# One transformer layer on one core: the pairs of a seven-product scheme in four stages instead of three, each engine's order rewritten, a fourth raw buffer, the residual in DRAM during the MLP

## The chip, the cores and the metric

The kernel runs on one core of a Trainium2 chip. A core has several engines that run their own queues side by side: TensorE (PE, matrix products; PEld is its loading of the stationary operand), VectorE (DVE), ScalarE (ACT), GpSimd (POOL) and SyncE (SP, which here issues the loads), with 16 DMA engines behind the queues. The metric is the device time of one execution in microseconds, as the median of several runs. A further execution is taken by the hardware profiler; its page and its trace are what the profile means below.

## The reference

One layer of a decoder on a sequence of 256 tokens of width 2048, all in float32: a block-sparse attention and a short convolution, merged by gates, then a squared-ReLU MLP, then a gated input embedding.

```python
D_MODEL = 2048; SEQ = 256; D_FF = 4 * D_MODEL
...
        r = r + merged @ w_o[i]
        h = rms_norm(r, g_mlp[i])
        r = r + jnp.square(jax.nn.relu(h @ w_up[i])) @ w_down[i]
        h = rms_norm(r, g_ple[i])
        r = r + jax.nn.sigmoid(h @ w_ple_gate[i]) * (p[i] @ w_ple_proj[i])
```

The change concerns the third line and what stands directly before and behind it: `w_up` is 2048 x 8192 and `w_down` 8192 x 2048.

## The kernel before

**Products in parts.** A float32 operand is split into a high part, which ACT rounds to the matmul's format (`hi`, a Copy), and a low part, which DVE gets by subtraction (`lo`). A product is hi·hi + hi·lo + lo·hi. So every weight passes through ACT and DVE before PE can use it, and a `lo` waits for its `hi` (`split`, L115 to L122). All operations go through four helpers, whose lines the profile shows: `act` L77, `mm` L80, `load` L83, DVE L87.

**Units.** The MLP works in 96 units of 1 MB of weights (128 x 2048 elements, as two halves of 128 x 1024). 64 are `up` units, one for each 128 columns of `w_up`; 32 are `dn` units, for the upper half of `w_down`'s output columns (tiles 8 to 15), in four groups of eight, one group for each quarter of the hidden width. A unit takes 32 matmuls (`cols`, L202): 15 of 512 columns, 16 of 256, and one more of 512. The order is 17 up, 8 dn, 16 up, 8 dn, 16 up, 8 dn, 15 up, 8 dn (`units`, L464 to L467). Units are numbered 0 to 95; the loop body that issues unit g's matmuls is called body g here.

**Pairs.** The other half of `w_down`'s work (output tiles 0 to 7) is done by a scheme of seven products instead of eight on 2 x 2 blocks. A pair j takes two hidden tiles, 2j and 2j + 1, as the blocks A11 to A22, and a raw tile `raw_s` with four blocks of `w_down`, B. From the A blocks come four sums S1 to S4 (`sum_u`, L539: four DVE operations on a quarter tile, then a split). From the B blocks come T1 to T4: `t13` is one DVE subtraction on a whole half tile, `t24` an addition and a subtraction. What is split are B11 with B22 (`b`), B21, T1 with T3 (`t13`), T2 with T4 (`t24`) and S. Each of the seven products is three matmuls, and all 32 pairs add up in seven banks of PSUM, 0 to 6, from the first pair to the last. So from unit 3 on all units use the one bank left, 7: unit g + 1 can start on PE once ACT has copied unit g's sums out of it (`evacuated`, L570: the instructions `up<-ps_up` and `dn<-ps_dn`).

**The preparation of a pair** has three parts (`split_part`, L508): part 0 splits `b`, forms and splits the S, and subtracts for `t13`; part 1 splits `t13`, forms `t24` and splits B21; part 2 splits `t24`. A table made ahead, `after` (L471 to L477), deals out one part to a body, two from body 88 on, each three units after the later of its hidden tiles at the earliest; the products of a part (two, two, three; `pair_part`, L555) follow the unit of the body it is dealt to.

**What sets the order.** From body 2 on ACT, DVE, PE and SP run the program in the order it is written (`keep_in_program_order`); POOL does too. A body g (L624 to L661) issues, in this order: the load of unit g + 3; the load of a pair where one begins in body g + 3; the matmuls of unit g; the split of the first half of unit g + 2; the finishing of unit g - 1 (`up_done`, L575: two DVE operations form `a`, ACT squares it, ACT and DVE split it into `x`; or `dn_done`, L589); the parts dealt to body g + 1; the split of the second half of unit g + 2; the evacuation of unit g; and the products of the parts dealt to body g. A load waits until one of three `raw` buffers (1 MB each, shared by units and pairs) is free, and the loads behind it on SP wait with it.

**The residual r** is held in eight tiles. After w_o four of them, tiles 0 to 3, are stored to DRAM (`r_kept`, L448), to make room, and come back behind the last product (L660). Tiles 4 to 7 stay in SBUF: a dn unit of the first three groups adds its two halves to them by two DMAs of POOL that accumulate in flight (L592), the second of which waits for the first. The last group adds on DVE. The small tiles (x, sums, evacuated sums, r) share a pool of 50 slots, `N_SLOT`; a slot is given again when its last reader is done, so an evacuation can come to wait for such a DMA. The seven `hi` and seven `lo` buffers of half a unit are shared by units and pairs alike.

Of the kernel before, what the change touches and what calls it, by code (L numbers as in the profile page):

```python
# [15 lines left out]
N_SLOT = 50  # L16
P = 128
S = 256
# [18 lines left out]
def hybrid_block_kernel(ctx: ExitStack, tc: tile.TileContext, ins: dict, out: bass.AP):  # L37
# [76 lines left out]

    def split(hi, lo, src, gain=None):  # L115
# [8 lines left out]
    def xsplit(xs, k, src, gain=None):  # L124

        x = slot([P, 2, S], F32R, "x")
        split(x[:, 0, :], x[:, 1, :], src, gain)
        xs[k] = x
# [18 lines left out]
    def load_unit(w):  # L147

        raw = wp.tile([P, UNIT], F32, tag="raw", name="raw", bufs=3)
        load(raw, w)  # L150
        return [split_half(raw[:, h * HALF:(h + 1) * HALF]) for h in range(2)]

    def load_half(w):
        raw = wp.tile([P, HALF], F32, tag="raw", name="raw", bufs=3)
        load(raw, w)
        return split_half(raw)

    def load_rows(w):

        raw = wp.tile([P, UNIT], F32, tag="raw", name="raw", bufs=3)  # L160
# [62 lines left out]
    def temp(name):  # L223
        return sm.tile([P, S], F32, tag="temp", name=name, bufs=8)
# [33 lines left out]
    def load_first(w):  # L258

        raw = wp.tile([P, UNIT], F32, tag="raw", name="raw", bufs=3)  # L260
# [144 lines left out]
    def split_m(n, ps):  # L405
        for i in range(2):
            xsplit(mT, n + i, ps[:, i, :])
# [33 lines left out]
    r_kept = [dram.tile([P, 2, S], F32, tag=f"r{u}", name=f"r_kept_{u}") for u in range(4)]  # L441
# [36 lines left out]
    assert not todo  # L478

    def load_raw(g):  # L480
        if g < NU:
            kind, i = units[g]
            w = ins["w_up"][i] if kind == "up" else ins["w_down"][16 * i[0] + i[1]]
            wU[g] = [wp.tile([P, UNIT], F32, tag="raw", name="raw", bufs=3)]
            load(wU[g][0], w)

    def split_unit(g, h):
        if g < NU:
            raw = wU[g][0]
            wU[g].append(split_half(raw[:, h * HALF:(h + 1) * HALF]))  # L490
# [12 lines left out]

    def both(w, names, hi, lo):
        for i, name in enumerate(names):
            w[name] = hi[:, i * CW:(i + 1) * CW], lo[:, i * CW:(i + 1) * CW]

    def split_part(j, i):  # L508


        w = wS[j]
        if i == 0:
            raw = w["raw"]
            hi, lo = half_tiles("b")
            flat = raw[:, 0:2, :].rearrange("p a f -> p (a f)")
            split(hi, lo, flat)
            both(w, ("B11", "B22"), hi, lo)
            sum_u(j)
            t = wp.tile([P, 2, CW], F32, tag="t", name="t13", bufs=2)
            dve.tensor_sub(t, raw[:, 0:2, :], raw[:, 2:3, :].to_broadcast([P, 2, CW]))  # L520
            w["t13"] = t
        elif i == 1:
            raw, t = w["raw"], w["t13"]
            hi, lo = half_tiles("t13")
            split(hi, lo, t.rearrange("p a f -> p (a f)"))
            both(w, ("T1", "T3"), hi, lo)
            t2 = wp.tile([P, 2, CW], F32, tag="t", name="t24", bufs=2)
            dve.tensor_add(t2[:, 0, :], raw[:, 1, :], t[:, 0, :])
            dve.tensor_sub(t2[:, 1, :], t2[:, 0, :], raw[:, 3, :])
            hi, lo = (slot([P, CW], F32R, f"b21_{n}") for n in range(2))  # L530
            split(hi, lo, raw[:, 3, :])
            w["B21"] = hi, lo
            w["t24"] = t2
        else:
            hi, lo = half_tiles("t24")
            split(hi, lo, w["t24"].rearrange("p a f -> p (a f)"))
            both(w, ("T2", "T4"), hi, lo)

    def sum_u(j):  # L539
# [7 lines left out]
        hi, lo = (slot([P, 4, P], F32R, f"s_{i}") for i in range(2))  # L547
        split(hi, lo, s)
        for i in range(4):
            sums[j, f"S{i + 1}"] = hi[:, i, :], lo[:, i, :]  # L550

    PRODUCTS = ((("P1", "A11", "B11"), ("P3", "S4", "B22")), (("P5", "S1", "T1"), ("P7", "S3", "T3")),
                (("P2", "A12", "B21"), ("P6", "S2", "T2"), ("P4", "A22", "T4")))

    def pair_part(j, i):  # L555

        for name, a, b in PRODUCTS[i]:
# [5 lines left out]
            else:  # L563
                xh, xl = sums[j, a]
# [10 lines left out]
    def up_done(k, st):  # L575

        a = temp("a")
        dve.tensor_add(a, st[:, :S], st[:, S:])
        dve.scalar_tensor_tensor(a, a, 0.0, row1, op0=ALU.max, op1=ALU.mult)
        act(a, a, AF.Square)  # L580
        u_raw[k] = a
        xsplit(uT, k, a)
# [6 lines left out]
    def dn_done(q, n, st):  # L589
        if q < 3:  # L590
            for i in range(2):
                nc.gpsimd.dma_start(r[n // 2][:, n % 2, :], st[:, i * S:(i + 1) * S], accum_op=ALU.add)  # L592
# [25 lines left out]
    for g in range(2):  # L618
        load_raw(g)
        for h in range(2):  # L620
            split_unit(g, h)
    load_raw(2)
    ended = False
    for g in range(NU):  # L624
# [5 lines left out]
        for j, part in after[min(g + 3, NU - 1)]:  # L630
            if part == 0 and j not in wS:
                load_pair(j)
        if kind == "up":
            ps = cols(wU[g][1:], hT, f"up_{i}")
        else:
            ps = cols(wU[g][1:], {k: uT[16 * i[0] + k] for k in range(16)}, f"dn_{i[0]}_{i[1]}")
# [4 lines left out]
        split_unit(g + 2, 0)  # L641
        for n in range(g) if g > 1 else ():
            if n in evac:
                k, m = units[n]
                up_done(m, evac.pop(n)) if k == "up" else dn_done(*m, evac.pop(n))
        if g + 1 < NU:
            for j, part in after[g + 1]:
                split_part(j, part)
        split_unit(g + 2, 1)
        evac[g] = evacuated(ps, kind)  # L650
        if kind == "up" and i == 63:
            up_done(i, evac.pop(g))
# [116 lines left out]
```

## Time and profile before

| | us |
|---|---|
| median of the runs (2 runs, 1612.8 to 1614.12) | 1613.46 |
| the profiled execution, its own time | 1610.67 |
| its span | 1608.9 |
| q, k, v | 0 to 147 of the span |
| convolution | 147 to 291 |
| gates and branches | 291 to 556 |
| w_o | 556 to 645 |
| MLP (96 units, 32 pairs) | 645 to 1503 |
| embedding gate | 1503 to 1609 |

The bounds of the stages are read off the timeline by the names of the tiles. The time of a run is a little longer than the span, which counts from the first instruction to the last. How busy an engine is on average over the span says little here, since the stages have different limits. For a stage one reads each engine's busy time in its window, then the waits within it (which engine waited for whose instruction, on which line), then the timeline of a few bodies. The granted clock belongs to the same window: the chip lowers PE's clock at times, and then the same matmuls take longer.

### The profile page before, as it was taken

Reading aid. Unit: us, or ns where it says so; the run is one execution under the profiler, and the core shown is the slowest. Engines: PE = TensorE matmul, PEld = TensorE weight load, DVE = VectorE, ACT = ScalarE, POOL = GpSimd, SP = SyncE. Lnnn points to the kernel's source line nnn. Section 1 sums busy time; section 2 is a strip of 40 time slices with the busy share of each in tenths; the row PEclk is TensorE's granted clock in tenths of the full one; section 3 lists DMA queues with packets and bytes.
Section 4 is the critical chain, followed back from the end, with each engine's and each line's share of the span. In section 5 each row is a group of like instructions: output and inputs, shape, how many; then the busy total and the mean of one; then the engine's idle time right before and its main releaser. Section 6 shows DMA issues by size and latency. Waiting matters only on the chain.

```text
span 1608.9 us, 19683 instructions
## 1 busy us (share of the span) xinstructions
PE 1488.1 (92%) x7528; PEld 1261.4 (78%) x7528; DVE 1053.3 (65%) x1547; ACT 820.3 (51%) x1280; POOL 56.8 (4%) x83
## 2 busy tenths in 40 slices
PE   8999999999999999888998888999889989777998
PEld 6888888888888888777787777877677877656887
DVE  7555777554655576667676667667666676766875
ACT  7655455545444454445554555545455454444653
POOL 0000000000000000000021000210001100000000
PEclk9999999999999999998999999999999989888999
DMA  8554454655555665353576545765357745444462
GB/s 314 209 184 166 175 176 166 206 186 187 195 194 184 234 213 204 106 183 131 184 211 176 164 136 171 208 191 179 135 162 203 212 135 179 131 136 158 165 206 76
DMA packets 133262, 286.80 MB, mean 178 GB/s; under 512 B 7472, under 2 KB 81456, under 8 KB 111152
## 3 DMA queue, kind: packets, MB, share of 16 engines
q1 hardware_dynamic: 125472, 277.11, 51.2%
q0 software_dynamic: 7552, 8.39, 3.0%
q8 instruction: 59, 0.97, 0.2%
q14 instruction: 35, 0.29, 0.1%
q10 hardware_dynamic: 144, 0.04, 0.0%
HBM read 276.08 MB, written 3.15 MB: 174 GB/s over the span
## 4 chain that ended last, share of the span: by engine, by line
PE 57%; DVE 15%; DMA 13%; ACT 8%; issue 5%; SPq 2%; DVEq 0%; ACTq 0%
PE ps_g L80 11%; PE ps_conv L80 8%; DMA raw<-in_w_up_dram 8%; PE ps_up L80 6%; PE ps_o L80 6%; PE ps_y L80 5%; DVE w_lo L87 5%; PE ps_pg L80 5%; PE ps_dn L80 5%; DMA raw<-in_w_down_dram 4%; ACT w_hi L77 3%; PE ps_k L80 3%; PE ps_v L80 3%; PE ps_q L80 2%; DVE b_lo L87 2%
## 5 line engine op out<-in xcount | busy, mean ns | idle before, releaser
L87 DVE TENSOR_TENSOR w_lo<-raw,w_hi 128x1024 fp32r<-128x1024 f32 (+1 forms) x556 | 556.6, 1023 | 372.2 <-ACT w_hi L77 291.6
L77 ACT ACTIVATE w_hi<-raw 128x1024 fp32r<-128x1024 f32 (+1 forms) x556 | 486.2, 892 | 332.1 <-PE ps_g L80 66.7
L80 PE MATMUL ps_up<-x,w_hi 128*128 128x512 f32 x1024 | 289.9, 431 | 75.6 <-ACT up L77 72.1
L80 PEld LDWEIGHTS ps_up<-x,w_hi 128*128 128x128 f32 x1024 | 213.5, 211 | 132.4 <-ACT up L77 83.1
L80 PE MATMUL ps_dn<-x,w_hi 128*128 128x512 f32 x512 | 140.7, 421 | 29.4 <-ACT dn L77 23.0
L80 PE MATMUL ps_g<-w_hi,x 128*128 128x512 f32 x512 | 159.1, 390 | 0.0
L80 PEld LDWEIGHTS ps_dn<-x,w_hi 128*128 128x128 f32 x512 | 103.8, 205 | 56.0 <-ACT dn L77 27.2
L80 PEld LDWEIGHTS ps_up<-x,w_lo 128*128 128x128 f32 x1024 | 131.3, 191 | 5.2
L80 PE MATMUL ps_up<-x,w_lo 128*128 128x256 f32 x1024 | 132.8, 283 | 0.0
L80 PEld LDWEIGHTS ps_g<-w_hi,x 128*128 128x128 f32 x512 | 96.1, 188 | 19.8
L77 ACT ACTIVATE a<-a 128x256 f32<-128x256 f32 x64 | 26.7, 418 | 153.0 <-DVE a L87 153.0
L80 PE MATMUL ps_g<-w_lo,x 128*128 128x512 f32 x256 | 99.6, 389 | 0.0
L87 DVE TENSOR_TENSOR t_lo<-t,t_hi 128x1024 fp32r<-128x1024 f32 x64 | 78.3, 1224 | 29.8 <-ACT t_hi L77 25.0
L80 PE MATMUL ps_conv<-x,w_hi 128*128 128x512 f32 x384 | 97.6, 397 | 0.0
L80 PEld LDWEIGHTS ps_conv<-x,w_hi 128*128 128x128 f32 x384 | 70.8, 188 | 13.3
L80 PE MATMUL ps_y<-w_hi,x 128*128 128x512 f32 x256 | 79.5, 389 | 0.0
L77 ACT ACTIVATE t_hi<-t 128x1024 fp32r<-128x1024 f32 x64 | 66.9, 1045 | 14.8 <-DVE t L87 12.5
L80 PE MATMUL P<-t_hi,s 128*128 128x512 f32 x192 | 70.2, 392 | 0.0
L80 PEld LDWEIGHTS ps_dn<-x,w_lo 128*128 128x128 f32 x512 | 65.6, 191 | 2.5
L80 PE MATMUL ps_dn<-x,w_lo 128*128 128x256 f32 x512 | 66.4, 283 | 0.0
L87 DVE TENSOR_TENSOR x<-a,x 128x256 fp32r<-128x256 f32 x64 | 27.2, 426 | 59.7 <-ACT x L77 59.7
L80 PE MATMUL ps_pg<-x,w_hi 128*128 128x512 f32 x256 | 64.4, 392 | 2.0 <-DVE x L87 2.0
(190 smaller groups left out, 2059.4 us busy)
## 6 DMA issues: line engine op xcount, KB each, us to landing
raw<-in_w_up_dram SPq DMA_DIRECT2D x64, 1024.0 KB, 5.3
raw<-in_w_in_dram SPq DMA_DIRECT2D x56, 1024.0 KB, 5.0
raw_s<-in_w_down_dram SPq DMA_DIRECT2D x128, 256.0 KB, 4.0
raw<-in_w_down_dram SPq DMA_DIRECT2D x32, 1024.0 KB, 6.4
raw<-in_w_qkv_dram SPq DMA_DIRECT2D x20, 1024.0 KB, 5.0
raw<-in_w_branch_dram SPq DMA_DIRECT2D x16, 1024.0 KB, 5.1
raw<-in_w_o_dram SPq DMA_DIRECT2D x16, 1024.0 KB, 4.9
raw<-in_w_ple_gate_dram SPq DMA_DIRECT2D x16, 1024.0 KB, 5.1
```

Of the source, the lines that this page charges most:

```text
L77: return inorder(nc.scalar.activation(*args, **kw))
L80: return inorder(nc.tensor.matmul(*args, **kw))
L87: return lambda *args, **kw: inorder(getattr(nc.vector, name)(*args, **kw))
```

## The change

- **Four stages.** A pair's preparation is dealt out in four stages (`stage`): 0 splits `b` and S; 1 subtracts for `t13` and splits it; 2 forms `t24` and splits B21; 3 splits `t24` and, in between, forms the S sums of the next pair (`sum_u(j + 1)`) where its hidden tiles are there. The products are 2, 2, 1 and 2.
- **Spread by kind.** Table `staged` gives an up body one stage (two in even bodies from 72 on) and a dn body two (three in every fourth, and from 88 on). The stages dealt to g are worked in body g and their products follow unit g + 1; before, the parts dealt to g + 1 were worked in body g.
- **Order in a body.** `up_done` is cut in three. On DVE the two operations that form `a` (`up_sum`) now stand ahead of the `lo` of the first half; on ACT the order is as before. The low part of `x` follows.
- **Raw buffers** are four instead of three. To make room, slots are 45 instead of 50, four of the tiles of `merged` ahead of w_o are held in the `t` buffers, and all eight r tiles go to DRAM behind w_o. `temp` has ten buffers instead of eight.
- **r in DRAM.** The 48 accumulating DMAs add into `r_kept`. In body 85 all eight tiles are loaded again.

The core of the diff:

```diff
-N_SLOT = 50
+N_SLOT = 45
...
-        raw = wp.tile([P, UNIT], F32, tag="raw", name="raw", bufs=3)
+        raw = wp.tile([P, UNIT], F32, tag="raw", name="raw", bufs=4)
...
-        return sm.tile([P, S], F32, tag="temp", name=name, bufs=8)
+        return sm.tile([P, S], F32, tag="temp", name=name, bufs=10)
...
+        room = wp.tile([P, 2, 2, S], F32R, tag="t", name="x_m", bufs=2) if n < 4 else None
         for i in range(2):
-            xsplit(mT, n + i, ps[:, i, :])
+            xsplit(mT, n + i, ps[:, i, :], room=None if room is None else room[:, i])
...
-            if n // 2 < 4:
-                nc.gpsimd.dma_start(r_kept[n // 2], r[n // 2])
+            nc.gpsimd.dma_start(r_kept[n // 2], r[n // 2])
...
-    todo = [(j, i) for j in range(32) for i in range(3)]
-    after = []
-    for g in range(NU):
+    todo = [(j, x) for j in range(32) for x in range(4)]
+    staged = []
+    for g in range(NU + 1):
+        kind = units[min(g, NU - 1)][0]
+        quota = (2 if g >= 72 and g % 2 == 0 else 1) if kind == "up" else 3 if g >= 88 or g % 4 == 0 else 2
         some = []
-        while todo and len(some) < (1 if g < 88 else 2) and up_at[2 * todo[0][0] + 1] + 3 <= g:
+        while todo and len(some) < quota and up_at[2 * todo[0][0] + 1] + 3 <= g:
             some.append(todo.pop(0))
-        after.append(some)
+        staged.append(some)
...
+    def stage(j, x):
...
+        if x == 0:
+            if j not in sums:
+                sum_u(j)
+            hi, lo = half_tiles("b")
...
+            return pieces(hi, lo, w["raw"][:, 0:2, :].rearrange("p a f -> p (a f)")) + pieces(sh, sl, s)
+        if x == 1:
...
+            first = [(False, lambda: dve.tensor_sub(t, raw[:, 0:2, :], raw[:, 2:3, :].to_broadcast([P, 2, CW])))]
+            return first + pieces(hi, lo, t.rearrange("p a f -> p (a f)"))
+        if x == 2:
...
+            part = pieces(hi, lo, raw[:, 3, :])
+            return part[:1] + [
+                (False, lambda: dve.tensor_add(t[:, 0, :], raw[:, 1, :], t13[:, 0, :])),
+                (False, lambda: dve.tensor_sub(t[:, 1, :], t[:, 0, :], raw[:, 3, :])),
+            ] + part[1:]
+        hi, lo = half_tiles("t24")
...
+        if j + 1 < 32 and 2 * j + 3 in u_raw:
+            part.insert(1, (False, lambda: sum_u(j + 1)))
+        return part
...
-                nc.gpsimd.dma_start(r[n // 2][:, n % 2, :], st[:, i * S:(i + 1) * S], accum_op=ALU.add)
+                nc.gpsimd.dma_start(r_kept[n // 2][:, n % 2, :], st[:, i * S:(i + 1) * S], accum_op=ALU.add)
...
+        if g == 85:
+            for u in range(8):
+                r[u] = slot([P, 2, S], F32, f"r_{u}")
+                nc.gpsimd.dma_start(r[u], r_kept[u])
...
-        split_unit(g + 2, 0)
...
-                up_done(m, evac.pop(n)) if k == "up" else dn_done(*m, evac.pop(n))
-        if g + 1 < NU:
-            for j, part in after[g + 1]:
-                split_part(j, part)
-        split_unit(g + 2, 1)
+        on_act, on_dve = unit_half(g + 2, 0)
+        on_act()
+        for n in done:
+            if units[n][0] == "up":
+                up_sum(units[n][1], evac.pop(n))
+        on_dve()
+        for k in ups:
+            up_high(k)
+        for k in ups:
+            up_low(k)
...
+        for j, x in stages(g):
+            for _, work in stage(j, x):
+                work()
+        for work in unit_half(g + 2, 1):
+            work()
         evac[g] = evacuated(ps, kind)
...
-        for j, part in after[g]:
-            pair_part(j, part)
+        for j, x in stages(g - 1):
+            products(j, x)
```

`pieces` gives a `hi` for ACT and a `lo` for DVE; `high` and `low` are the two halves of `split`; `unit_half` is one half of a unit's split.

In the rows below a name is the tile's, with a running number; the arrow goes from the inputs to the output. DVE's order before, in body 30, an up body that works the first part of pair 9:

```order
L87 TENSOR_TENSOR w_lo_7539<-raw_7441,w_hi_7538 128x1024
L87 TENSOR_TENSOR a_7542<-up_7495 128x256
L87 SCALAR_TENSOR_TENSOR a_7542<-a_7542,rstd_row_mlp_5566 128x256
L87 TENSOR_TENSOR x_7546<-a_7542,x_7546 128x256
L87 TENSOR_TENSOR b_lo_7550<-raw_s_7369,b_hi_7549 128x1024
L87 TENSOR_TENSOR s_raw_7553<-a_7330,a_7411 128x128
L87 TENSOR_TENSOR s_raw_7553<-s_raw_7553,a_7330 128x128
L87 TENSOR_TENSOR s_raw_7553<-a_7330 128x128
L87 TENSOR_TENSOR s_raw_7553<-a_7411,s_raw_7553 128x128
L87 TENSOR_TENSOR s_1_7559<-s_raw_7553,s_0_7558 128x512
L87 TENSOR_TENSOR t13_7562<-raw_s_7369 128x1024
L87 TENSOR_TENSOR w_lo_7565<-raw_7441,w_hi_7564 128x1024
```

And the last rows of DVE's body 31 and the whole of body 32 after the change, where pair 9 begins:

```order
L87 TENSOR_TENSOR s_raw_7606<-a_7396,s_raw_7606 128x128
L87 TENSOR_TENSOR t24_lo_7604<-t24_7538,t24_hi_7603 128x1024
L87 TENSOR_TENSOR w_lo_7613<-raw_7487,w_hi_7612 128x1024
L87 TENSOR_TENSOR a_7659<-up_7616 128x256
L87 SCALAR_TENSOR_TENSOR a_7659<-a_7659,rstd_row_mlp_5567 128x256
L87 TENSOR_TENSOR w_lo_7657<-raw_7557,w_hi_7656 128x1024
L87 TENSOR_TENSOR x_7664<-a_7659,x_7664 128x256
L87 TENSOR_TENSOR b_lo_7668<-raw_s_7489,b_hi_7667 128x1024
L87 TENSOR_TENSOR s_1_7670<-s_raw_7606,s_0_7669 128x512
L87 TENSOR_TENSOR w_lo_7676<-raw_7557,w_hi_7675 128x1024
```

The two rows of `a` have moved ahead of `w_lo`; the four rows of `s_raw` stand a body earlier, ahead of `t24_lo`; `t13` has moved to the next body.

ACT's order before, in a dn stretch (bodies 43 to 45, one part in each), between two evacuations and the next:

```order
L77 ACTIVATE dn_8483<-ps_dn_1_10_8429 128x512
L77 ACTIVATE w_hi_8526<-raw_8422 128x1024
L77 ACTIVATE t24_hi_8532<-t24_8472 128x1024
L77 ACTIVATE w_hi_8536<-raw_8422 128x1024
L77 ACTIVATE dn_8540<-ps_dn_1_11_8493 128x512
L77 ACTIVATE w_hi_8583<-raw_8491 128x1024
L77 ACTIVATE b_hi_8589<-raw_s_8424 128x1024
L77 ACTIVATE s_0_8598<-s_raw_8593 128x512
L77 ACTIVATE w_hi_8604<-raw_8491 128x1024
L77 ACTIVATE dn_8608<-ps_dn_1_12_8550 128x512
```

After the change, in body 44, a dn body with three stages:

```order
L77 ACTIVATE dn_8427<-ps_dn_43_8371 128x512
L77 ACTIVATE w_hi_8481<-raw_8369 128x1024
L77 ACTIVATE t24_hi_8487<-t24_8416 128x1024
L77 ACTIVATE b_hi_8496<-raw_s_8293 128x1024
L77 ACTIVATE s_0_8498<-s_raw_8490 128x512
L77 ACTIVATE t13_hi_8505<-t13_8504 128x1024
L77 ACTIVATE w_hi_8510<-raw_8369 128x1024
L77 ACTIVATE dn_8514<-ps_dn_44_8448 128x512
```

Between two evacuations stand now six instructions instead of three or four, among them three of pairs.

POOL's order around the first dn group, before and after: the target of the accumulating DMAs.

```order
L592 DMA r_4_4616<-dn_6687 128x256 x2
L592 DMA r_4_4616<-dn_6755 128x256 x2
L592 DMA r_5_4618<-dn_6827 128x256 x2
L592 DMA r_5_4618<-dn_6884 128x256 x2
L592 DMA r_6_4620<-dn_6952 128x256 x2
```

```order
L621 DMA r_kept_4_4627<-dn_6627 128x256 x2
L621 DMA r_kept_4_4627<-dn_6702 128x256 x2
L621 DMA r_kept_5_4628<-dn_6771 128x256 x2
L621 DMA r_kept_5_4628<-dn_6858 128x256 x2
L621 DMA r_kept_6_4629<-dn_6930 128x256 x2
```

Their number and order are the same; the target is the copy in DRAM.

More of the change, by code (lines that the diff above doesn't have):

```diff
@@ L122, in split, with xsplit @@
             dve.scalar_tensor_tensor(lo, src, gain, hi.bitcast(F32), op0=ALU.mult, op1=ALU.subtract)
-    def xsplit(xs, k, src, gain=None):
-        x = slot([P, 2, S], F32R, "x")
+    def xsplit(xs, k, src, gain=None, room=None):
+        x = slot([P, 2, S], F32R, "x") if room is None else room
         split(x[:, 0, :], x[:, 1, :], src, gain)
@@ L440, in hybrid_block_kernel @@
     ss1 = slot([P, 2, S], F32, "ss1")
-    r_kept = [dram.tile([P, 2, S], F32, tag=f"r{u}", name=f"r_kept_{u}") for u in range(4)]
+    r_kept = [dram.tile([P, 2, S], F32, tag=f"r{u}", name=f"r_kept_{u}") for u in range(8)]
     for n in range(16):
@@ L502, in load_pair @@
         wS[j] = {"raw": raw}
[L504 to L537, printed above, removed]
     def sum_u(j):
@@ L552, in hybrid_block_kernel, with products @@
     PRODUCTS = ((("P1", "A11", "B11"), ("P3", "S4", "B22")), (("P5", "S1", "T1"), ("P7", "S3", "T3")),
-                (("P2", "A12", "B21"), ("P6", "S2", "T2"), ("P4", "A22", "T4")))
-    def pair_part(j, i):
-        for name, a, b in PRODUCTS[i]:
+                (("P2", "A12", "B21"),), (("P6", "S2", "T2"), ("P4", "A22", "T4")))
+    def products(j, x):
+        for name, a, b in PRODUCTS[x]:
             if j == 0:
@@ L573, in evacuated, with up_sum, up_high, up_low @@
         return st
-    def up_done(k, st):
-        a = temp("a")
+    def up_sum(k, st):
+        a = u_raw[k] = temp("a")
         dve.tensor_add(a, st[:, :S], st[:, S:])
         dve.scalar_tensor_tensor(a, a, 0.0, row1, op0=ALU.max, op1=ALU.mult)
-        act(a, a, AF.Square)
-        u_raw[k] = a
-        xsplit(uT, k, a)
+    def up_high(k):
+        act(u_raw[k], u_raw[k], AF.Square)
+        uT[k] = slot([P, 2, S], F32R, "x")
+        high(uT[k][:, 0, :], u_raw[k])
+    def up_low(k):
+        low(uT[k][:, 1, :], u_raw[k], uT[k][:, 0, :])
     def enter_ple(u):
@@ L620, in hybrid_block_kernel @@
         for h in range(2):
-            split_unit(g, h)
+            for work in unit_half(g, h):
+                work()
     load_raw(2)
@@ L629, in hybrid_block_kernel @@
         load_raw(g + 3)
-        for j, part in after[min(g + 3, NU - 1)]:
-            if part == 0 and j not in wS:
+        for j, x in stages(g + 2):
+            if x == 0:
                 load_pair(j)
[L633 to L636, printed above, removed]
+        if g == 85:
+            for u in range(8):
+                r[u] = slot([P, 2, S], F32, f"r_{u}")
+                nc.gpsimd.dma_start(r[u], r_kept[u])
+        xs = hT if kind == "up" else {k: uT[16 * i[0] + k] for k in range(16)}
+        ps = cols(wU[g][1:], xs, f"{kind}_{g}")
         if g == 0:
@@ L640, in hybrid_block_kernel @@
             row1 = rstd_rows(rstd1, "mlp")
-        split_unit(g + 2, 0)
-        for n in range(g) if g > 1 else ():
-            if n in evac:
-                k, m = units[n]
-                up_done(m, evac.pop(n)) if k == "up" else dn_done(*m, evac.pop(n))
-        if g + 1 < NU:
-            for j, part in after[g + 1]:
-                split_part(j, part)
-        split_unit(g + 2, 1)
+        done = [n for n in range(g) if n in evac] if g > 1 else []
+        ups = [units[n][1] for n in done if units[n][0] == "up"]
+        on_act, on_dve = unit_half(g + 2, 0)
[8 more added lines that the diff above has]
+            up_low(k)
+        for n in done:
+            if units[n][0] == "dn":
+                dn_done(*units[n][1], evac.pop(n))
+        for j, x in stages(g):
+            for _, work in stage(j, x):
+                work()
+        for work in unit_half(g + 2, 1):
+            work()
         evac[g] = evacuated(ps, kind)
         if kind == "up" and i == 63:
-            up_done(i, evac.pop(g))
-        for j, part in after[g]:
-            pair_part(j, part)
-        if not ended and prod and all(not a for a in after[g + 1:]):
+            up_sum(i, evac.pop(g))
+            up_high(i)
+            up_low(i)
+        for j, x in stages(g - 1):
+            products(j, x)
+        if not ended and prod and not any(staged[g:]):
             ended = True
             end_products()
-            for u in range(4):
-                r[u] = slot([P, 2, S], F32, f"r_{u}")
-                nc.gpsimd.dma_start(r[u], r_kept[u])
         run_pending(1)
```

55 lines of the change are left out of this document (41 added, 14 removed).

## The prediction

> **What bounds the kernel now.** I read the page first, then busy times by stage, then the waits and the timeline of the stage that stands out. TensorE is the bound (busy time on the page), and the first two windows below (gates with branches, then w_o) show it without a gap at full clock. The third, the MLP, has 858 us with 750 busy at a mean granted clock of 0.93 (columns: length, then busy time of PE, PEld, DVE, ACT and POOL, clock, DMA share, GB/s).
>
> ```profile
> PE 1488.1 (92%) x7528; PEld 1261.4 (78%) x7528; DVE 1053.3 (65%) x1547; ACT 820.3 (51%) x1280; POOL 56.8 (4%) x83
> ...
> 291.00:556.00 265.00, 265.00 (x1182) 219.64 (x1181) 144.62 (x228) 127.39 (x219) 0.00 (x0) 1.00 0.60 199
> 556.00:645.00 89.00, 89.00 (x516) 78.38 (x515) 62.59 (x89) 43.08 (x57) 2.35 (x4) 1.00 0.59 200
> ...
> 645.00:1503.00 858.00, 749.97 (x3783) 632.13 (x3781) 584.26 (x817) 431.64 (x598) 43.99 (x53) 0.93 0.53 167
> ```
>
> So the change acts on the stage with the slack. DVE is busy 584 us of 858 and ACT 432: neither is full, and yet the waits of this stage are hand-offs between them (who waited for whom: total us, times, longest):
>
> ```profile
> ACT a L77 <- DVE a L87: 153.0, 64, 3.4
> DVE w_lo L87 <- ACT w_hi L77: 127.0, 52, 6.0
> POOL r L592 <- DMA r<-dn: 126.3, 24, 10.1
> ...
> ACT s L77 <- DVE s_raw L87: 74.4, 32, 3.4
> ...
> PE ps_up L80 <- ACT up L77: 72.1, 23, 6.0
> ...
> ACT w_hi L77 <- DMA raw<-in_w_up_dram: 50.0, 22, 3.9
> ...
> ACT w_hi L77 <- DMA raw<-in_w_down_dram: 32.5, 14, 5.0
> ...
> PE ps_dn L80 <- ACT dn L77: 23.0, 10, 7.2
> ```
>
> All units share accumulator bank 7, so a unit cannot start before ACT has evacuated the one before (72.1 and 23.0 us), and ACT comes late to that evacuation because it stood in its fixed order behind DVE (153 and 74 us) and behind a late load (50 and 32.5). A body here is one turn of the loop over the 96 units; the timeline shows the end of body 30 and the three after it:
>
> ```profile
> 898.36 1.06 ACT L77 ACTIVATE w_hi<-raw 128x1024 fp32r<-128x1024 f32 x1 [3.81 <-DMA raw<-in_w_up_dram]
> ...
> 901.51 0.42 ACT L77 ACTIVATE a<-a 128x256 f32<-128x256 f32 x1 [2.09 <-DVE a L87]
> ...
> 905.54 0.63 ACT L77 ACTIVATE s<-s_raw 128x512 fp32r<-128x512 f32 x1 [2.22 <-DVE s_raw L87]
> ...
> 907.02 0.58 ACT L77 ACTIVATE up<-ps_up 128x512 f32<-128x512 f32 x1
> ...
> 907.65 6.18 PE L80 MATMUL ps_up<-x,w_hi 128*128 128x512 f32 x15 [5.14 <-ACT up L77]
> ...
> 916.01 0.60 ACT L77 ACTIVATE up<-ps_up 128x512 f32<-128x512 f32 x1 [1.60 <-PE ps_up L80]
> ...
> 917.19 3.56 PE L80 MATMUL ps_up<-x,w_hi 128*128 128x512 f32 x15
> ...
> 919.64 0.42 ACT L77 ACTIVATE a<-a 128x256 f32<-128x256 f32 x1 [2.09 <-DVE a L87]
> ...
> 922.50 0.40 PE L80 MATMUL ps_up<-x,w_hi 128*128 128x512 f32 x1
> ...
> 922.74 0.40 PE L80 MATMUL P<-t_hi,s 128*128 128x512 f32 x1
> ...
> 922.93 0.60 ACT L77 ACTIVATE up<-ps_up 128x512 f32<-128x512 f32 x1 [0.53 <-PE ps_up L80]
> ...
> 924.12 3.56 PE L80 MATMUL ps_up<-x,w_hi 128*128 128x512 f32 x15
> ...
> 935.13 0.58 ACT L77 ACTIVATE up<-ps_up 128x512 f32<-128x512 f32 x1
> ```
>
> Three waits in a row (3.81, 2.09, 2.22) bring the evacuation to 907.02; PE stood 5.14 us, and its next 15 matmuls took 6.18 us where an undisturbed unit needs 3.56. Three units on, the evacuation is at 935.13: 28.1 us for the three bodies that carry one pair. PE itself needs 917.19 to 922.74 = 5.55 us for a unit and 922.74 to 924.12 = 1.38 for six product matmuls, 0.23 each, 0.69 a product (three matmuls): 3 x 5.55 + 7 x 0.69 = 21.5.
>
> **The change, part by part.** Products, units and bytes stay the same; the gain can only be idle time of PE and the slow matmuls behind it. The terms are taken between four evacuations of the trace (units 0, 6, 86 and 93):
>
> ```profile
> 650.62 0.60 ACT L77 ACTIVATE up<-ps_up 128x512 f32<-128x512 f32 x1 [2.58 <-PE ps_up L80]
> 701.40 0.58 ACT L77 ACTIVATE up<-ps_up 128x512 f32<-128x512 f32 x1
> 1387.13 0.60 ACT L77 ACTIVATE up<-ps_up 128x512 f32<-128x512 f32 x1 [0.53 <-PE ps_up L80]
> 1478.60 0.60 ACT L77 ACTIVATE dn<-ps_dn 128x512 f32<-128x512 f32 x1 [2.67 <-PE ps_dn L80]
> ```
>
> *Four stages, fixed order and fourth raw buffer together.* Prices of single operations (busy us, mean ns of one, idle before), and the loads of w_down (median us to landing):
>
> ```profile
> L87 DVE TENSOR_TENSOR w_lo<-raw,w_hi 128x1024 fp32r<-128x1024 f32 x193 | 232.2, 1221 | 143.1 <-ACT w_hi L77 127.0 <-PE ps_dn L80 9.8 <-PE ps_up L80 4.0
> L77 ACT ACTIVATE w_hi<-raw 128x1024 fp32r<-128x1024 f32 x193 | 202.4, 1049 | 104.4 <-DMA raw<-in_w_up_dram 50.0 <-DMA raw<-in_w_down_dram 32.5 <-PE ps_dn L80 18.2
> ...
> L87 DVE TENSOR_TENSOR x<-a,x 128x256 fp32r<-128x256 f32 x64 | 27.2, 426 | 59.7 <-ACT x L77 59.7
> ...
> L87 DVE TENSOR_TENSOR s<-s_raw,s 128x512 fp32r<-128x512 f32 x32 | 22.1, 692 | 22.3 <-ACT s L77 22.3
> ...
> L87 DVE TENSOR_TENSOR s_raw<-a 128x128 f32<-128x128 f32 x64 | 18.2, 284 | 0.0
> ...
> raw<-in_w_down_dram SPq DMA_DIRECT2D x32, 1024.0 KB, 6.4
> ```
>
> Each body splits one unit: two w_hi on ACT (2.1 us) and two w_lo on DVE (2.44). A pair adds on DVE four large passes (1.22 each), four of half size (0.69) and four of a quarter (0.28): 8.8 us; an up unit adds three like x's (0.43). Over four up bodies with one pair DVE has 4 x 3.7 + 8.8 = 23.6 us; PE has 4 x 5.55 + 7 x 0.69 = 27.0. DVE is thus hidden, and ACT (432 us in the stage) more so, if neither stands behind the other. The edits see to that: the addition of a unit's result comes ahead of w_lo on DVE, so the 2.09 us ahead of `a` are covered by a w_hi that ACT has in hand; sum_u goes a body ahead, so the 2.22 us ahead of `s` vanish; t13's subtraction and its split share a stage and wait for each other, but nothing else stands there. The waits on raw loads (50 + 32.5) go in the up stretches, where a fourth buffer lets a load start two bodies or more ahead of its use instead of one. In dn stretches, with two or three stages a body, a load starts some 7 us ahead by the order, against a landing of 6.4, so some will be late: between 0 and the 32.5 us of before I take 6, near the lower end, since a landing beyond 7 is the exception.
>
> What stays: a body without products (six: 27, 28, 51, 52, 75, 76) shows the evacuation to PE. The unit's last matmul starts at 922.50 and the next could follow at 922.74, but the evacuation ends at 922.93 + 0.60 = 923.53: about 0.83 us each with the hand-over. A stage with one product (eleven) covers 0.69 of that and shows 0.16. A dn body with three stages keeps ACT at split work past the unit's end, 1.1 us by adding the rows up, six times, and 9 us with its neighbours; an up body with two stages 0.6, five times.
>
> - Units 0 to 6: 50.8 us before; 6 x 5.55 + 4 x 0.69 + 2 for the first waits = 38. Saves 12.
> - Units 6 to 86: 685.7 before. 80 x 5.55 = 444, 191 products x 0.69 = 132, exposures 5 + 2 + 9 + 3 = 19: 595. Saves 91.
> - Units 86 to 93: 91.5 before. 7 x 5.55 + 28 x 0.69 = 58, and 12 for four bodies with three stages and two with two, in which DVE and ACT are the bound: 70. Saves 21.
> - Before unit 0 and behind unit 93: the same work in the same order; 0.
>
> Sum 124 us saved, and 118 with the 6 for late loads in the dn stretches.
>
> *r in DRAM.* The 48 accumulating transfers now add into DRAM; the first of a unit's two must land before the second goes out, and a later evacuation needs its slot back (unit 21's waits for the transfers of unit 19, 45's for 43's, 69's for 67's). Rows: the issues of all 48 (min/median/max ns), the landings of the first group of eight units, then the median landings of all 48 and of the plain copies:
>
> ```profile
> L592 POOL DMA_DIRECT2D r<-dn x48: 840/849/1192, 799.1 to 1267.8; - x48
> ...
> DMA to landing us min/median/max: 2.6/6.4/10.7
> ...
> r<-dn POOLq DMA_DIRECT2D x48, 128.0 KB, 4.7
> ...
> r_kept<-r POOLq DMA_DIRECT2D x4, 256.0 KB, 5.0
> r<-r_kept POOLq DMA_DIRECT2D x4, 256.0 KB, 3.5
> ```
>
> The longest wait of POOL for its own transfers (10.1, above) goes with the longest landing (10.7), so a wait is about L - 0.6, and with two issues of 0.85 a unit holds the queue L + 1.1 us. Eight dn bodies last 8 x 5.55 + 31.5 products x 0.69 = 66 us in the new order. A group therefore loses 8 x (L + 1.1) - 66, nothing below L = 7.15. Ends: 4.7 costs nothing; 10.7 costs 28 per group, 85 in three. No row shows a target in DRAM being added to. The nearest is the first group's 6.4, and I take 1 us on top: 7.4, 2 per group, 6 in all. A gain is excluded, since nobody waited for these transfers before but POOL itself.
>
> The Trainium skill's page "DMA: Bandwidth & Descriptors", section "Anatomy of one DMA — SWDGE (gpsimd) path", speaks against this edit: the fixed part of such a transfer is mostly the receipt of the write, which "can cause a surprisingly long delay especially when the write target is HBM". Its fit would give an estimate of 2.3 us for 128 KB, and a sum with no loss; no row shows which of the two holds for an add into DRAM, and the rows above, all of them longer than that fit, come nearer to the warning.
>
> *The rest.* Four more stores of r during w_o and four more reloads (3.5 to 5.0 us each) lie on POOL, which is nearly idle; w_o's PE is full at a DMA share of 0.59. The x tiles in the t buffers, ten temp buffers and 45 slots move no work. 0 us.
>
> 118 - 6 = 112. The profiled execution took 1610.67 us; 1610.67 - 112 = 1498.7. The median of the runs, 1613.46, is 2.8 above it: **1501**.
>
> **Rivals.**
> - *A slow add into DRAM.* The chain is transfer, slot, evacuation of a dn unit, PE. At L = 10 a group loses 23 us, 68 in all: 1613 - 118 + 68 = 1563. For it: the queue was in backlog already (126.3 us of POOL waiting for its own transfers). Against it: a plain store of twice the size into DRAM landed in 5.0.
> - *Hand-offs stay.* If ACT keeps about half of the 2.09 us per up unit on the way to the evacuation, 64 x 1.05 = 67 come back: 1613 - 112 + 67 = 1568. For it: a body has 8 to 12 hand-offs between ACT and DVE in fixed order. Against it: body 32 above, where `a` was waited for just as long (919.64) and PE ran on, from 917.19 to 924.12 without a stop.
> - *No change.* If memory is the bound of the MLP and not the order, the order gains nothing: 1613. For it: loads are waited for, at 167 GB/s. Against it: 199 and 200 GB/s in the two stages ahead at a DMA share of 0.60 and 0.59; the MLP in 858 - 112 = 746 us would need 167 x 858 / 746 = 192.
> - *Slower*, by the add into DRAM alone: the saving is gone when a group loses 39, at L = 12.1; 2% more is lost at 50 per group, L = 13.4: 1646. That is above the longest landing in the trace.
>
> **How the numbers follow.** About 2% of the time (32 us: below 1581, above 1646) can be told from no change. The forecast with its unknown up to 1530 has 0.68; DRAM at L about 10 or the hand-offs 0.17, also faster; no change 0.09; slower 0.06. So faster 0.85, same 0.09, slower 0.06. The range goes down to 1470 (no loss to DRAM or to late loads, 1613 - 124 = 1489, and the 19 us of exposures hidden) and up to 1570, which takes in the two moderate rivals, so that little more than the last two cases, 0.15, and the edges are left out.
>
> **What would show it.** Right: in the new trace the wait of PE for the evacuation under 30 us in the MLP, `a` and `s` waited for on ACT by less than a third of before, evacuations 27 us per four up bodies, clock near 1.00. Wrong: evacuations of dn units that wait for a transfer of POOL (L above 8 us); `w_hi` still waiting for raw loads by 50 us or more; per-pair time of 28 us or more in four up bodies while PE idles.

## The result, and the profile after

The changed kernel takes 1495.57 us (median of 2 runs, 1493.7 to 1497.43) against 1613.46 before: a ratio of 0.9269, 95% interval 0.9217 to 0.9322. The prediction was 1501. The span fell from 1608.9 to 1495.7, by 113.2 us where 112 had been worked out.

First the engines over the span and the MLP's window after the change (length, busy time of PE, PEld, DVE, ACT and POOL, clock, DMA share, GB/s):

```profile
PE 1452.7 (97%) x7528; PEld 1239.2 (83%) x7528; DVE 1050.5 (70%) x1547; ACT 822.8 (55%) x1280; POOL 61.1 (4%) x91
```

```profile
645.00:1391.00 746.00, 713.99 (x3785) 609.01 (x3783) 582.81 (x820) 435.60 (x601) 46.65 (x58) 0.98 0.62 193
```

The MLP shrank from 858 to 746 us. DVE and ACT did the same work in it as before (584 and 432 us there, 583 and 436 here). PE's busy time fell from 750 to 714 although its matmuls are the same ones: fewer of them ran at the lowered clock (0.93 before, 0.98 now). The other 76 us were PE's idle time. Its waits, and those of the two engines that feed it, in the same window:

```profile
ACT up L77 <- PE ps_up L80: 116.2, 56, 5.8
POOL r_kept L621 <- DMA r_kept<-dn: 108.0, 24, 8.6
ACT t_hi L77 <- DVE t L87: 102.3, 41, 4.7
...
PE ps_dn L80 <- ACT dn L77: 19.8, 8, 3.4
...
ACT a L77 <- DVE a L87: 10.4, 18, 1.6
...
PE ps_up L80 <- ACT up L77: 8.5, 10, 3.0
...
ACT s L77 <- DVE s_raw L87: 5.0, 7, 0.7
```

PE's waits for an evacuation fell from 72.1 + 23.0 to 8.5 + 19.8. In up bodies it is now ACT that stands ready and waits for PE (116.2 us, 56 times); that is the sign that PE has become the bound there. `a` fell from 153 to 10.4 and `s` from 74 to 5. No wait of `w_hi` for a raw load is left in the stage (82.5 before). One wait has grown: ACT for `t13` and `t24`, which DVE forms (the view leaves the numbers of the tiles out). It was 102.3 us after the change, against this before:

```profile
ACT t_hi L77 <- DVE t L87: 12.5, 4, 4.8
```


The four evacuations from which the prediction's terms were taken, after the change:

```profile
650.91 0.60 ACT L77 ACTIVATE up<-ps_up 128x512 f32<-128x512 f32 x1 [2.58 <-PE ps_up L80]
688.89 0.60 ACT L77 ACTIVATE up<-ps_up 128x512 f32<-128x512 f32 x1 [2.53 <-PE ps_up L80]
1290.40 0.60 ACT L77 ACTIVATE up<-ps_up 128x512 f32<-128x512 f32 x1 [2.96 <-PE P L80]
1367.12 0.60 ACT L77 ACTIVATE dn<-ps_dn 128x512 f32<-128x512 f32 x1 [2.68 <-PE ps_dn L80]
```

| stretch | before | after | saved | worked out |
|---|---|---|---|---|
| units 0 to 6 | 50.8 | 38.0 | 12.8 | 12 |
| units 6 to 86 | 685.7 | 601.5 | 84.2 | 91, less 12 for DRAM and late loads |
| units 86 to 93 | 91.5 | 76.7 | 14.8 | 21 |
| the rest of the span | 780.9 | 779.5 | 1.4 | 0 |

A pair's four up bodies look like this (timeline of PE and ACT, start and length):

```profile
907.41 0.60 ACT L77 ACTIVATE up<-ps_up 128x512 f32<-128x512 f32 x1 [1.69 <-PE ps_up L80]
...
914.34 0.60 ACT L77 ACTIVATE up<-ps_up 128x512 f32<-128x512 f32 x1 [0.55 <-PE ps_up L80]
...
916.06 0.42 ACT L77 ACTIVATE a<-a 128x256 f32<-128x256 f32 x1 [0.17 <-DVE a L87]
...
921.26 0.60 ACT L77 ACTIVATE up<-ps_up 128x512 f32<-128x512 f32 x1 [2.87 <-PE ps_up L80]
...
928.19 0.60 ACT L77 ACTIVATE up<-ps_up 128x512 f32<-128x512 f32 x1 [2.61 <-PE ps_up L80]
...
934.72 0.60 ACT L77 ACTIVATE up<-ps_up 128x512 f32<-128x512 f32 x1 [1.69 <-PE ps_up L80]
```

Every evacuation waits for PE, and the four bodies between the first row and the last take 934.72 - 907.41 = 27.3 us, against 27.0 of pure matmul time and 28.1 for three bodies before.

### The profile page after: what moved, and what is told of

It reads as the page before. It is cut to its first block, busy times and chain, and to the rows that moved or that the text cites. A ratio compares the mean times of both kernels' runs of the same rounds, so it can differ in the third digit from the quotient of the medians.

```text
span 1495.7 us, 19751 instructions
## 1 busy us (share of the span) xinstructions
PE 1452.7 (97%) x7528; PEld 1239.2 (83%) x7528; DVE 1050.5 (70%) x1547; ACT 822.8 (55%) x1280; POOL 61.1 (4%) x91
## 4 chain that ended last, share of the span: by engine, by line
PE 93%; DVE 2%; ACT 2%; issue 1%; DMA 1%; SPq 0%; ACTq 0%; DVEq 0%
PE ps_up L80 23%; PE ps_g L80 12%; PE ps_dn L80 11%; PE ps_conv L80 9%; PE P L80 9%; PE ps_o L80 6%; PE ps_y L80 6%; PE ps_pg L80 6%; PE ps_q L80 3%; PE ps_k L80 3%; PE ps_v L80 3%; ACT w_hi L77 1%; PE ps_proj L80 1%; DMA raw<-in_w_down_dram 1%; DVE t L87 1%
## 5 line engine op out<-in xcount | busy, mean ns | idle before, releaser
L80 PE MATMUL ps_up<-x,w_hi 128*128 128x512 f32 x1024 | 257.8, 394 | 8.5 <-ACT up L77 8.5
L80 PEld LDWEIGHTS ps_up<-x,w_hi 128*128 128x128 f32 x1024 | 191.9, 189 | 52.9 <-ACT up L77 16.1
L80 PE MATMUL ps_dn<-x,w_hi 128*128 128x512 f32 x512 | 137.9, 415 | 19.8 <-ACT dn L77 19.8
L77 ACT ACTIVATE t_hi<-t 128x1024 fp32r<-128x1024 f32 x64 | 67.6, 1056 | 109.9 <-DVE t L87 102.3
L80 PEld LDWEIGHTS ps_g<-w_hi,x 128*128 128x128 f32 x512 | 96.1, 188 | 19.8
L77 ACT ACTIVATE up<-ps_up 128x512 f32<-128x512 f32 x64 | 38.1, 595 | 119.2 <-PE ps_up L80 116.2
L87 DVE TENSOR_TENSOR a<-up 128x256 f32<-128x256 f32 x64 | 27.1, 423 | 51.6 <-ACT up L77 51.6
```

Source lines behind the costliest of these rows:

```text
L77: return inorder(nc.scalar.activation(*args, **kw))
L80: return inorder(nc.tensor.matmul(*args, **kw))
L87: return lambda *args, **kw: inorder(getattr(nc.vector, name)(*args, **kw))
```

## The experiments

The change has three parts that the prediction had costed as one: the memory (fourth raw buffer, with r in DRAM, slots and temp buffers as its price), the order on DVE, and the deal of stages. The runs take them apart. Two theories stood against each other: H, the hand-offs between ACT and DVE carried most of the gain; L, the late loads did. Times are medians of four runs or more (two for the changed kernel); a ratio is to the kernel before, run beside it on the same chip. The kernel before took 1611.0 to 1613.8 us beside the experiments, so a difference between kernels that were not run beside each other is good to some 3 us. Of a longer diff only the telling lines are shown.

**e1_three_raw**: the buffer taken away from the changed kernel.

```diff
-        raw = wp.tile([P, UNIT], F32, tag="raw", name="raw", bufs=4)
+        raw = wp.tile([P, UNIT], F32, tag="raw", name="raw", bufs=3)
...
```

> The changed kernel with three raw buffers instead of four, all else as changed. Theory H (the hand-offs between ACT and DVE carried most of the gain of 118 us): the order still holds, and only late loads come back, at most part of the 82 us for which ACT waited for them before: 1500 to 1540 us. Theory L (the loads carried it, and the order only moved work about): most of the gain is lost, 1570 us or more, and ACT's waits of w_hi for raw loads return to 60 us or more.

1582.44 us, ratio 0.9817 (0.9797 to 0.9837). L's number: 87 us of the gain of 118 are gone. The loads are waited for again in the MLP, as the waits of this run say:

```profile
ACT w_hi L77 <- DMA raw<-in_w_down_dram: 65.3, 17, 6.4
...
ACT w_hi L77 <- DMA raw<-in_w_up_dram: 36.6, 13, 5.8
```

But they aren't where the prediction had put them. The windows of units 28 to 40 (up) and 40 to 48 (dn), first in this run, then in the changed kernel:

```profile
876.66:958.20 81.54, 80.89 (x442) 69.80 (x443) 66.00 (x97) 52.03 (x76) 0.00 (x0) 1.00 0.57 194
958.20:1045.33 87.13, 70.56 (x346) 58.90 (x344) 54.22 (x70) 38.80 (x48) 11.95 (x14) 0.92 0.60 166
```

```profile
853.19:934.72 81.53, 80.89 (x442) 69.80 (x443) 66.96 (x97) 51.99 (x76) 0.00 (x0) 1.00 0.58 194
934.72:1003.54 68.82, 66.35 (x343) 56.37 (x342) 53.72 (x70) 38.93 (x49) 11.09 (x13) 0.98 0.74 208
```

Twelve up bodies take 81.5 us with three buffers and with four. The dn group takes 87.1 instead of 68.8. In a dn stretch of the new deal the loads for a unit and, every second body, for a pair share the buffers. With three of them a load is issued only about when ACT is ready for it (timeline, dn body 42 of e1_three_raw):

```profile
966.30 3.56 PE L80 MATMUL ps_dn<-x,w_hi 128*128 128x512 f32 x15
...
966.85 1.48 SPq L83 DMA_DIRECT2D raw<-in_w_down_dram  x2
972.04 1.06 ACT L77 ACTIVATE w_hi<-raw 128x1024 fp32r<-128x1024 f32 x1 [6.32 <-DMA raw<-in_w_down_dram]
...
976.81 0.58 ACT L77 ACTIVATE dn<-ps_dn 128x512 f32<-128x512 f32 x1
...
977.44 6.33 PE L80 MATMUL ps_dn<-x,w_hi 128*128 128x512 f32 x15 [3.37 <-ACT dn L77]
```

ACT stands 6.32 us before the split, the evacuation is late by it, PE idles 3.37 us, and its next 15 matmuls take 6.33 us instead of 3.56. Of the 86 us between the two profiled spans, 67 lie in the three dn groups up to unit 73 and 20 in units 76 to 93.

**e2_three_raw_sbuf**: the same, and the add goes into SBUF again, with 49 slots and four tiles of r kept there.

```diff
-                nc.gpsimd.dma_start(r_kept[n // 2][:, n % 2, :], st[:, i * S:(i + 1) * S], accum_op=ALU.add)
+                nc.gpsimd.dma_start(r[n // 2][:, n % 2, :], st[:, i * S:(i + 1) * S], accum_op=ALU.add)
...
```

> As e1_three_raw, and the accumulating DMAs add into r tiles in SBUF again (four tiles kept there, 49 slots, four reloads). It isolates the target of the add. If the add into DRAM costs nothing (its landing after the change was 3.9 us in the median against 4.7 into SBUF before): within 5 us of e1_three_raw. If it costs what the prediction put in, 6 us, or more: faster than e1_three_raw by 6 us or more.

1576.52, ratio 0.9791 (0.9762 to 0.982), 5.9 below e1 in the median. That is at the edge of the expectation, the intervals overlap, and the two profiled spans are 1581.8 (e2) and 1581.5 (e1): undecided by this run alone.

**e6_before_dram**: r in DRAM as the only change to the kernel before; the diff is that of e2 the other way round, with eight stores and eight reloads.

> The kernel before with r in DRAM alone: eight stores, the accumulating DMAs add into DRAM, eight reloads in body 85; three raw buffers, 50 slots and the old order stay. If an add into DRAM is no slower than one into SBUF: within 8 us of the kernel before. If it were slow (landing above 7 us): 1620 to 1660.

1613.54, ratio 1.0007 (0.9989 to 1.0025). By the interval an add into DRAM costs at most 4 us here, and the medians show no cost. Median landings, in this run and then in the changed kernel:

```profile
r_kept<-dn POOLq DMA_DIRECT2D x48, 128.0 KB, 4.4
```

```profile
r_kept<-dn POOLq DMA_DIRECT2D x48, 128.0 KB, 3.9
```

Into SBUF it was 4.7 before. The fair pair is 4.7 and 4.4, since nothing but r differs there; with three raw buffers it is 3.4 into SBUF (e2) and 3.5 into DRAM (e1).

**e7_before_rooms**: the kernel before with the whole changed memory, its own parts, table and order.

```diff
-N_SLOT = 50
+N_SLOT = 45
...
-        raw = wp.tile([P, UNIT], F32, tag="raw", name="raw", bufs=3)
+        raw = wp.tile([P, UNIT], F32, tag="raw", name="raw", bufs=4)
...
-        return sm.tile([P, S], F32, tag="temp", name=name, bufs=8)
+        return sm.tile([P, S], F32, tag="temp", name=name, bufs=10)
...
```

> The kernel before, with its three parts, table and order, and the changed memory alone: r in DRAM, four raw buffers, 45 slots, ten temp buffers. e1_three_raw lost 87 us when the fourth buffer was taken away. Theory L (the buffer carries the gain by itself): 1510 to 1550. Theory H (the buffer is needed, but so is the order: loads were one of three waits in a row ahead of an evacuation, and the two behind DVE remain): 1560 to 1595.

1527.39, ratio 0.9463 (0.9435 to 0.9492): 86 us faster with the old order untouched. L again. The waits of this run hold the lesson (no wait of `w_hi` for a raw load is among them any more):

```profile
ACT a L77 <- DVE a L87: 166.6, 64, 3.4
...
ACT s L77 <- DVE s_raw L87: 72.8, 32, 2.4
...
PE ps_up L80 <- ACT up L77: 31.9, 34, 6.0
```

The two waits that headed the prediction's list, for `a` and for `s`, are about as long as before (153 and 74 there), and yet three quarters of the gain are there. With the load's wait gone from the head of the row, most of the other two falls beside PE's own work: between the evacuations of units 0 and 93 PE idled 105 us in the kernel before and 50 here. Where the 83 us between the two profiled spans lie is another matter than in e1: 60 of them in up bodies, 22 in the dn groups.

**e11_before_three**: e7 with three raw buffers, to tell the buffer from the other memory.

> As e7_before_rooms (the kernel before with the changed memory: r in DRAM, 45 slots, ten temp buffers), but with three raw buffers. If the fourth raw buffer alone made e7_before_rooms 86 us faster: within 8 us of the kernel before. If a part came from the ten temp buffers or the slots: between 1535 and 1600.

1613.59, ratio 1.0023 (1.0005 to 1.004). The temp buffers, the slots and r in DRAM bring nothing (by the interval they cost 1 to 6 us); the 86 us are the fourth raw buffer's.

**e3_lo_first** and **e4_sums_in_stage**: one edit of DVE's order undone at a time, with four buffers; and **e5_both**, both undone. Below is the edit of e3, then a part of e4's, which also puts the sums behind the split of `b` in stage 0.

```diff
+        on_dve()
         for n in done:
             if units[n][0] == "up":
                 up_sum(units[n][1], evac.pop(n))
-        on_dve()
```

```diff
-        if j + 1 < 32 and 2 * j + 3 in u_raw:
-            part.insert(1, (False, lambda: sum_u(j + 1)))
...
```

> The changed kernel, but on DVE the low part of the unit's first half stands ahead of the addition that forms a again, as before. H: ACT waits for a by some 2 us in each of 64 up bodies again (130 us in all), but ACT now waits for PE by 2.1 us in the mean body at the evacuation, so that most is taken up: 0 to 30 us more, 1496 to 1526. If this order alone carried the gain: 1560 or more. L: no change.

> The changed kernel, but the S sums are formed in stage 0 itself, between the split of b and their own split, as before. H: ACT waits for s by some 2 us in each of 32 stage-0 bodies, where the evacuation has only 0.2 to 0.6 us to spare: 1.5 us more for each of some 21 pairs in up bodies, more in dn bodies with several stages, 1525 to 1545 in all. L: no change, 1496.

> The changed kernel with both orders on DVE put back, the low part ahead of a and the S sums inside stage 0; four stages, four raw buffers and their spread stay. e3_lo_first cost 30 us and e4_sums_in_stage 40. If each is a wait of its own in front of the evacuation, they add: 1560 to 1580. If they cover each other (whoever waits for the one has the other by then): 1535 to 1550.

e3: 1525.68, ratio 0.9469 (0.9443 to 0.9495), 30 us slower than the change, at the end of H's range. e4: 1535.62, 0.9526 (0.9507 to 0.9545), 40 slower, as H had it. e5: 1592.8, 0.9868 (0.9838 to 0.9898), 97 slower, more than the sum of 70. So the expectation was too low for e5. Between the evacuations of units 0 and 93 e5 loses 31 us more than e3 and e4 together. 16 of them are idle time of PE; that both waits use the same slack ahead of the evacuation would explain it, but no run shows it directly. The other 15 are slower matmuls: PE's busy time there is 688 us in the changed kernel, 697 in e3 and in e4, and 721 in e5. e5 is also 65 us slower than e7, which has the same memory and has the low part and the S sums at the same places on DVE. Four stages dealt out by kind are worse than the old three parts unless the order goes with them. The opposite case, the new order on DVE with the old three parts, was not run.

**e10_same_rate**: the changed kernel with the stages dealt alike to up and dn bodies.

```diff
-        quota = (2 if g >= 72 and g % 2 == 0 else 1) if kind == "up" else 3 if g >= 88 or g % 4 == 0 else 2
+        quota = 3 if g >= 88 else 2 if g % 3 == 1 else 1
```

> The changed kernel with its stages dealt to up and dn bodies alike, four to every three bodies (2, 1, 1), which is the rate of pairs that the kernel before had; from body 88 on three as in the changed kernel. It undoes the spread by kind alone. If this spread matters (an up body has no room on DVE for more than one stage): 1515 us or more. If the order is what matters: a two-stage up body took 8.3 us after the change (bodies 77 to 78) against 7.97 on PE, and the dn groups lose their bodies of 11 us, so 1480 to 1500.

1517.73, ratio 0.9404 (0.9374 to 0.9433): 22 us slower than the change, so the spread by kind matters; the guess for the case where it doesn't was too low. Up bodies 28 to 40, which carry four pairs here, take 92.7 us against 66.6 + 28 x 0.69 = 85.9 on PE; with three pairs, in the changed kernel, 81.5 against 81.1. Of the up bodies only those with one stage hide it wholly.

**e8_two_per_dn** and **e9_even**: two deals that the theory of the three-stage body suggests. e8 drops the third stage in dn groups; e9 gives two stages to every body from 76 on as well. The diff is that of e9.

```diff
-        quota = (2 if g >= 72 and g % 2 == 0 else 1) if kind == "up" else 3 if g >= 88 or g % 4 == 0 else 2
+        quota = (2 if g >= 76 else 1) if kind == "up" else 2
```

> The changed kernel with two stages in every dn body up to 88; the third in every fourth is left out and falls into the up bodies behind the group that had no stage (bodies 25 to 27 and their like). By the theory that the three-stage body in the middle of a group loses some 6 us (bodies 44 and 45: 22.7 us against 15.9 on PE) and the bodies without products some 0.8 each: 18 to 24 us less, 1472 to 1478. If the 6 us come from the dn stretch as such (buffers shared by unit and pair), they only move: within 6 us of the changed kernel, 1490 to 1500.

> As e8_two_per_dn, and from body 76 on two stages in every body, up or dn, so that no body has three and the last stages end a body earlier. Units 75 to 93 took 162 us after the change. At 8.3 to 8.4 us for a two-stage up body (as in e10_same_rate) and 8.0 for a two-stage dn body they would take some 150: 10 to 14 us below e8_two_per_dn, 1460 to 1468. If two up bodies with two stages in a row make DVE the bound (3.7 + 4.4 = 8.1 us of work in each, and no light body to catch up): 9 us a body, no better than e8_two_per_dn.

e8: 1476.24, ratio 0.9147 (0.9108 to 0.9186). e9: 1464.12, ratio 0.9076 (0.9044 to 0.9107), faster than both kernels, by some 31 us than the change. Both totals came as expected. In e9 the way there was partly another: units 75 to 93 took 156 us, not 150 (the two-stage bodies went 9.1 and 7.5 in turn, and the dn bodies 88 to 91 took 7.5 to 11.0), and 8 us more were gained behind unit 93, since the products end a body earlier (119 us from there to the end, against 127 in e8). PE is busy in nearly the whole MLP now (window as above):

```profile
645.00:1361.00 716.00, 704.66 (x3795) 605.30 (x3795) 583.61 (x825) 437.85 (x606) 46.79 (x58) 1.00 0.64 200
```

**e12_even_three**: e9 with three raw buffers.

> As e9_even, the fastest so far, with three raw buffers. In e1_three_raw the up stretches ran at PE's pace with three buffers (81.5 us for units 28 to 40) and the dn groups lost 18 us each and more. If the dn groups need the buffer for the two loads of a pair's and a unit's data in every second body, whatever the spread: 60 to 90 us over e9_even, 1525 to 1555, with up stretches at 82 us again. If the loss came only with the three-stage bodies: under 1500.

1542.96, ratio 0.9567 (0.9531 to 0.9603): 79 us slower. Up bodies 28 to 40 take 81.9 us, as in e9; the dn group of units 40 to 48 takes 79.0 against 62.7. The buffer is needed by the dn stretches and the tail in both deals.

## Why the prediction was right, point by point

**The bound.** Right. The slack was the MLP's, the gain is idle time of PE and the slow matmuls behind it, and all other stages kept their time.

**Buffer, order and stages together.** The sum was right, its inner split was not told, and its reason stood on the wrong foot. The prediction led with the hand-offs (`a` 153 us, `s` 74 us) and let the loads follow. The runs give, one step upon the other: memory without the buffer 0 (e11), the fourth buffer 86 (e7), order and stages at the old rate 10 (e10 against e7, whose intervals are just apart), the spread by kind 22 (the change against e10). From the other side, without the buffer everything else is worth 29 (e1). So the buffer is worth 86 to 87 and the rest 29 to 32. That the two ways agree is in part chance, since the 86 us lie in other places each time. The step that failed is "The waits on raw loads (50 + 32.5) go in the up stretches, where a fourth buffer lets a load start two bodies or more ahead": in the new order the up stretches need no fourth buffer (81.5 us with three), and it is the dn stretches and the tail that do. In the old order, with a pair in every three bodies, the up stretches gain most from it (units 28 to 40: 111.2 before, 96.1 in e7; 60 of 83 us in all). The rest, 29 to 32, isn't the price of the hand-offs either: order and stages were never run apart with the old deal, and with the new deal the order alone is worth 97 us (e5).

**Late loads left in dn stretches: 6.** Measured 0; no wait of `w_hi` for a load is left in the MLP. The reason given, that a landing beyond 7 us is the exception, was a misreading: before the change 12 of the 32 loads of w_down landed later than that, and 6 after it. In the changed trace the tightest load of a unit landed 0.7 us ahead of its split, so the 0 is partly luck.

**r in DRAM: 6, L = 7.4.** Measured 0 within some 4 us (e6), and L = 3.9 in the median after the change (4.4 in e6). The mechanism, that long landings would reach an evacuation through its slot, did not come into play: 3 of the 48 landings after the change were above the 7.15 from which a group was to lose (the longest 9.1), and no evacuation waited for one. The Trainium skill's page "DMA: Bandwidth & Descriptors" warns in its section on the SWDGE path of a long delay with HBM as the target; for these 128 KB adds the traces don't show it: 4.4 us into DRAM in e6, 4.7 into SBUF before.

**Three-stage bodies: 1.1 us each, 9 with their neighbours; tail: 12.** Right in kind, too small in size. Units 6 to 86 show 601.5 - 444 - 132 = 25.5 of exposures instead of 19, and units 86 to 93 show 76.7 - 58.2 = 18.5 instead of 12. By body and at the prediction's own prices, the three-stage body in the middle of a group and its neighbours lose 12.7 us in the three groups, the ones at the end of a group nothing, and the six bodies without products 9.8 instead of 5. In the middle body DVE reaches `t13`'s subtraction late, ACT waits 4.09 us for it, the evacuation is late and PE idles 2.46 us, not 1.1. First these two rows of ACT in body 20, then PE's stall behind bodies 20, 44 and 68 (15 matmuls, idle time before):

```profile
788.65 1.06 ACT L77 ACTIVATE t_hi<-t 128x1024 fp32r<-128x1024 f32 x1 [4.09 <-DVE t L87]
...
790.55 0.58 ACT L77 ACTIVATE dn<-ps_dn 128x512 f32<-128x512 f32 x1
```

```profile
791.18 3.74 PE L80 MATMUL ps_dn<-x,w_hi 128*128 128x512 f32 x15 [2.46 <-ACT dn L77]
968.94 5.29 PE L80 MATMUL ps_dn<-x,w_hi 128*128 128x512 f32 x15 [2.46 <-ACT dn L77]
1148.24 5.04 PE L80 MATMUL ps_dn<-x,w_hi 128*128 128x512 f32 x15 [2.46 <-ACT dn L77]
```

Two of the three also paid some 1.5 us for a lowered clock (granted 0.68 during the second row, 1.00 during the first), which the prediction hadn't put behind a stall so short. Taking the third stage away (e8) saved 19 us, the bodies without products included: units 6 to 86 show 5.8 us of exposures there.

**The whole.** 12 us that were set aside for DRAM and late loads weren't needed, and some 13 more were lost to crowded bodies than worked out. The two errors cancel by luck; 1501 is therefore nearer to 1495.6 than its terms were. The signs named beforehand came true (PE's waits for evacuations 28.3 us, `a` 10.4, `s` 5.0, 27.3 us per four up bodies, clock 0.98). But they can't tell the two theories apart: in e7 `a` and `s` are waited for as long as ever, and the kernel is 86 us faster.

**The rivals.** *Slow add into DRAM*, and with it *slower*: refuted by e6. *Hand-offs stay*: refuted in the changed kernel (`a` 10.4 us); e3, e4 and e5 show the price had one or both stayed, 30, 40 and 97 us, where 67 had been worked out for half of the waits for `a`. *No change because memory is the bound*: refuted, at 193 GB/s after the change and 200 in e9. What the fourth buffer cured was loads that started late, not a lack of rate.

## What to carry to other kernels

A row of waits ahead of one instruction isn't costed by the length of each. Here the wait for loads (82 us) was worth 86, and everything else in the change, the two hand-offs (153 and 74 us) included, some 30 on top of it. The worth of a part also depends on the rest: put back into the changed kernel, the two hand-offs cost 97. So undo each part alone, from both ends, before giving it the credit.

When work is dealt to bodies of different kinds, cost each body by its most crowded engine chain, not by the group's sum: the dn group had enough room on every engine and still lost time in its one body with three stages. And a buffer is to be counted in the order that will run, where loads of two kinds meet: the same fourth buffer gained most in the up stretches of the old order and in the dn groups of the new one.

## What the runs showed of the hardware

**The clock falls behind shorter stalls than expected, and not always.** In the MLP of the fourteen traces, 15 matmuls that start right behind an idle time of PE of 1.0 to 1.87 us took 3.7 us; behind 1.88 to 3.71 us some took 3.7 and others 5.0 us or more (the three rows of 2.46 above are one case); behind more than 3.73 us all took 5.0 us or more. The shortest stall with slow matmuls is in e5:

```profile
710.27 5.31 PE L80 MATMUL ps_up<-x,w_hi 128*128 128x512 f32 x15 [1.89 <-ACT up L77]
```

The granted clock in these 5.3 us was 0.68. The Trainium skill's page "TensorE: Matmul & The Clock Gate", Part 1, puts the fall to the lower clock after an idle window of about 3.4 us and says that the window is free-running; that one length of stall has both outcomes fits the second, and the rows show that a stall of 1.9 us can already be enough. So a stall of 1.8 us cost 1.8 here, one of 1.9 to 3.7 us cost itself and in most cases 1.3 to 2.9 us more.

**An add in flight into DRAM is no slower than one into SBUF**, at 128 KB and beside the loads of this kernel (167 GB/s over the MLP before): 4.4 us in e6 against 4.7 before, in the median.
